# Transposing softmax weights as two halves, moving rows of maxima in one transfer, and planning with other issue times, in a two-layer diffusion transformer

## The chip, the cores and the metric

The kernel runs on one core of a Trainium2 chip. Its time is the device time of one execution in microseconds (us); of several runs the median is given. The engines work in parallel, each through its own instruction stream in order: TensorE (PE, matrix products), VectorE (DVE), ScalarE (ACT, exponentials and copies), GpSimd (POOL, here subtractions and small powers), and SyncE (SP), which in this kernel issues every DMA transfer. The 16 DMA engines then move the data.

## The reference

`BATCH` is 1, `SEQ` 1024 tokens on a 16 x 64 grid, 256 context tokens, width 1024, 16 heads of 64. Layer 0 is grouped-query attention with normed, rotated queries and keys; layer 1 is attention over a window of 8 x 16 neighbours with a learned bias. Each mixer's output is multiplied by a SiLU gate before its output projection. Cut to what this case touches, layer 0 computes, for each block of 128 queries:

```python
q = apply_axial_rope(rms_norm(q, q_g), cos, sin)
k = apply_axial_rope(rms_norm(k, k_g), cos, sin)
k_all = jnp.concatenate([kc, k], axis=1)      # 256 context keys, 1024 token keys
v_all = jnp.concatenate([vc, v], axis=1)
s = jnp.einsum('bqkgd,bskd->bkgqs', qi, k_all).astype(jnp.float32) * ATTN_SCALE
p = jax.nn.softmax(s, axis=-1).astype(v_all.dtype)
o = jnp.einsum('bkgqs,bskd->bqkgd', p, v_all)
yx = (o * jax.nn.silu(z)) @ w_out
```

The input norms are scaled so that scores are large, and a softmax needs the maximum of each query's row before its exponential.

## The kernel before

**Numbers as pairs.** Nearly every operand of a product is kept as two float16 tensors, a high half (the value rounded) and a low half (what the rounding left). A product is then three matmuls: high by high, high by low, low by high.

**Layer 0.** The 16 heads are worked in 8 pairs u. A pair's queries come in five blocks b of two 128-token tiles, and attention in three parts pt: tiles 0 to 3, tiles 4 to 7, and the two context tiles. For pairs 0 to 5 (`QH`) the two heads of a pair take different ways through the token tiles:

- Head 0 (`a_att`) computes scores already transposed, keys by queries (tiles `st`, L1204 and L1205), so that their exponentials (`ph`, `pf` on ACT, the low half `pl` on POOL) are the weights for the value product without a transpose. A query's maximum must then be subtracted inside the product: row 64 of the tile `q2` holds 3 minus the maximum, and row 64 of `k2` holds ones. `mgen` computes the maxima from scores of the high halves (L997, L998), and `rows` brings them into that row: it reduces the partial maxima (L1019), negates them into columns of `zmax` (L1022), transposes that tile by DMA into `zt` (L1023), so that each query tile's maxima are one row of `zt`, and copies rows of `zt` into `q2` (L1027, one transfer per query tile, where only head 0 needs them; L1029, one transfer for all, in the other cases). PE's second score product (L1205) waits for these rows.
- Head 1 (`q_att`) computes scores queries by keys (tile `qs`, L1137 and L1138), so the maximum is a plain reduction (L1140, L1144, L1145). Per query tile t, ACT writes the high half of the weights for 1024 keys into blocks 0 to 7 of the tile `qpp` (L1147) and the exact exponential into `qpf` (L1148); `p_split` writes the low half, their difference, into blocks 8 to 15 on POOL (L1066) or, every sixth time, on VectorE (L1063). One DMA transpose brings the 16 blocks of 128 x 128 into `qpt` (L1151). The value products (L1125 with the high half, L1127 with the low half, alternating key tile by key tile) follow. The 256 context keys go by `qcp` and `qct` (L1154, L1160), four tiles together.

`qpp`, `qpt`, `qcp` and `qct` share six buffers (`y_tile`, tag Y1). Names in the order listings carry u, pt and t: `qpt101` is pair 1, part 0, tile 1; `q211` and `zt11` belong to pair 1, part 1.

**Layer 1** projects queries, keys, values and gates by a scheme of seven products (L1503, L1505), and its window attention transposes weights of 8 or 10 blocks per head and tile (`bph` to `bpht`, L1643).

**What sets the order.** The program text only fixes what depends on what. The class `Planner` then reads all instructions, gives each a cost (`cost`: how long it holds its engine, and how much later its result is there), plays the program through with these costs, and repeats that with due times worked back from PE's stream. The order it ends with is fixed on every engine, SP's queue included; at run time each engine works through its list and waits where an operand is late. For a DMA transpose the cost was 1340 ns of SP whatever its size, and a data time in proportion to its elements.

Of the kernel before, what the change touches and what calls it, by code (L numbers as in the profile page):

```python
# [24 lines left out]
NX = 8  # L25
# [24 lines left out]
class Planner:  # L50
# [42 lines left out]
    def cost(self, x, rd, wr):  # L93
# [4 lines left out]
        n = max([self.elems(a) for a in outs + ins] or [1])  # L98
# [12 lines left out]
        if k == "InstDmaTransposeAnt":  # L111
            m = 1
            for s, c in list(ins[0].ap):
                m *= c
            return 1340.0, m / 128 * 23.4 / 16
        if k == "InstDMACopy":
            m = 1
            for s, c in list(outs[0].ap):
# [391 lines left out]
def trunk_kernel(ctx, tc, x, cx, cc, ng_row, w_mod, w_mod0, b_mod, a_qz, a_kv, a_qg, a_kg, a_w_out,  # L510
                 b_in, tab, b_w_out, fin_g, ones, cos_t, sin_t, out):
    nc = tc.nc
    V, S, G, T, DM = nc.vector, nc.scalar, nc.gpsimd, nc.tensor, nc.sync
# [184 lines left out]
    def y_tile(shape, dt, name, j, at=None):  # L698

        if j == 0:  # L700
            ny[0] += 1
            return main.tile(list(shape), dt, name=name, tag=f"Y0{ny[0] % 2 if at is None else at}", bufs=1)
        return main.tile(list(shape), dt, name=name, tag="Y1", bufs=6)
# [156 lines left out]
    for kt in range(KT):  # L860
# [8 lines left out]
        for t in ((0, 2) if kt < 2 else (0,)):  # L869
            n = 2 if kt < 2 else 4  # L870
# [73 lines left out]
    def a_proj(u, at):  # L944
# [62 lines left out]
        def rows(pts):  # L1007

            zm = zmax[nrow[0] % len(zmax)]
            nrow[0] += 1  # L1010
            zf = aq.tile([P, 16], F32, name=f"zf{u}{pts[0]}", tag="zf", bufs=2)
            zt = aq.tile([P, P], F16, name=f"zt{u}{pts[0]}", tag="zt", bufs=2)
            c0, outs = 0, []
            for pt_ in pts:
                mxs, n = pairs[(u, pt_)][3], PTN[pt_]
                hs = (0,) if pt_ < 2 and u in QH else (0, 1)
                zv = zf[:, c0:c0 + n * len(hs)].rearrange("p (t h) -> p t h", h=len(hs))
                for i in hs:
                    V.tensor_reduce(zv[:, :, i], mxs[i] if pt_ < 2 else mxs[i][:, 0:n, 2:3], axis=AX.X, op=ALU.max)  # L1019
                outs.append((c0, n, len(hs), pairs[(u, pt_)][1]))  # L1020
                c0 += n * len(hs)
            V.tensor_scalar(zm[:, 0:c0], zf[:, 0:c0], -1.0, CSH, op0=ALU.mult, op1=ALU.add)  # L1022
            DM.dma_start_transpose(zt, zm)  # L1023
            for c, n, h, q2 in outs:
                for t in range(n) if h == 1 else (None,):
                    if h == 1:
                        DM.dma_start(q2[64:65, t, 0, :], zt[c + t:c + t + 1])  # L1027
                    else:
                        DM.dma_start(q2[64:65], zt[c:c + n * h])  # L1029
            yield 200  # L1030

        items = []
        for b in range(NT // 2):
            m = (1100 if u in QH else 2200) if b < 4 else 440
            if u == 0:
                v, w, vp, vm, mw = FIRST[b]
            else:
                v = at + 0.2 * b
                w, vp, vm, mw = 0.2, v + 0.29, v + 0.31, 0.2 * m / (1100 if u in QH else 2200)
            items.append((mm(b), v, v + w, 5120))  # L1040
            items.append((post(b), vp, vp + 0.01, 220))
            items.append((mgen(b), vm, vm + mw, m))
            if b in (1, 4):
                items.append((rows((0,) if b == 1 else (1, 2)), vm + mw + 0.01, vm + mw + 0.02, 400))
# [67 lines left out]
    def q_att(u, pt_):  # L1112

        q1, q2, sz, _ = pairs[(u, pt_)]
# [14 lines left out]
        for t in range(4):  # L1129
# [16 lines left out]
            pp = y_tile((P, 2 * NX, P), F16, f"qpp{nm}", 1)  # L1146
# [1 line left out]
            S.activation(pf, pf, AF.Exp, bias=nmx, accum_out=sums[:, t, 0:1])  # L1148
            p_split(pp[:, 0:NX], pp[:, NX:2 * NX], pf, 6)
            ppt = y_tile((P, 2 * NX, P), F16, f"qpt{nm}", 1)  # L1150
            DM.dma_start_transpose(ppt, pp.rearrange("p a b -> p (a b)"))  # L1151
            S.activation(cp[:, t, 0:2], pfc, AF.Exp, bias=nmx)
            S.activation(pfc, pfc, AF.Exp, bias=nmx, accum_out=sums[:, t, 1:2])
            G.tensor_tensor(cp[:, t, 2:4], pfc, cp[:, t, 0:2], op=ALU.subtract)  # L1154
# [787 lines left out]
```

## Time and profile before

| What | Value |
|---|---|
| Runs | 1323.93, 1319.07, 1318.21 us; median 1319.07 us |
| Profiled execution | 1312.96 us, its span 1311.2 us |
| PE busy | 1281.5 us, 98% of the span |
| DVE, ACT, POOL busy | 1025.2, 893.9, 807.4 us |
| DMA | 211.40 MB in 431610 packets; 71.4% of 16 engines' span |
| Granted TensorE clock | 0.999 |

Layer 0's attention lies between about 100 and 640 us of the span, its output projection and the change of layers up to about 800 us, layer 1's attention up to about 1200 us, and the output after that. "Busy" of PE counts a matmul from its start to its modelled end, and matmuls overlap, so short gaps between them do not show. A row of the waits has the waiting instruction, what released it, the total in us, how often, and the longest. SP's transfers appear in the order in which they were issued, with the time of the issue alone; the data land later. Rows of the listings name a tile without its number, so `q<-zt` is a transfer from `zt` into `q2`.

### The profile page before, as it was taken

To read this page: it belongs to the slowest core of one execution; us is meant where nothing else is said; L and a number is where in the kernel's file an instruction comes from. 1 tells how busy PE (TensorE), PEld (TensorE's weight loads), DVE (VectorE), ACT (ScalarE), POOL (GpSimd) and SP (SyncE) were. 2 spreads that over 40 slices of the span, in tenths; PEclk is the share of its full clock that TensorE was granted. 3 is DMA by queue.
4 is the path that set the end of the run, shared out by engine and by line. 5 is a ranking of instruction groups with operands and counts; after the bars stand their busy time and mean duration, and the time that the engine had idled before them with its cause. 6 is when DMAs were issued, how large, how long until landed. Compare 5 with 4: busy or idle time off the path is not lost. (4 is left out here: it accounts for less than half of the span.)

```text
span 1311.2 us, 37092 instructions
## 1 busy us (share of the span) xinstructions
PE 1281.5 (98%) x14503; PEld 899.9 (69%) x14503; DVE 1025.2 (78%) x2410; ACT 893.9 (68%) x1835; POOL 807.4 (62%) x1030
## 2 busy tenths in 40 slices
PE   9999999999999999999999999999999999999997
PEld 6458777777777777767654466778696777868543
DVE  4787788798979798969658896778888788788743
ACT  3672797788878887778864345777878677777611
POOL 1572787677687876768864883556665555553432
PEclk9999999999999999999999999999999999999999
DMA  9422478778788886884406795789798887979923
GB/s 371 162 82 72 99 142 167 134 179 170 140 161 184 153 164 145 168 213 124 137 34 181 209 165 175 136 172 182 148 182 167 165 188 138 195 155 236 244 97 113
DMA packets 431610, 211.40 MB, mean 161 GB/s; under 512 B 386697, under 2 KB 390601, under 8 KB 431433
## 3 DMA queue, kind: packets, MB, share of 16 engines
q1 hardware_dynamic: 431434, 209.04, 71.4%
q8 instruction: 113, 1.85, 0.6%
q14 instruction: 63, 0.52, 0.1%
HBM read 97.23 MB, written 14.71 MB: 85 GB/s over the span
## 5 line engine op out<-in xcount | busy, mean ns | idle before, releaser
L1066 POOL TENSOR_TENSOR pl<-pf,ph 128x256 f16<-128x256 f32 x340 | 239.4, 728 | 66.6 <-ACT pf L1191 51.8
L1066 POOL TENSOR_TENSOR bph<-bpf,bph 128x256 f16<-128x256 f32 (+1 forms) x172 | 148.9, 890 | 184.4 <-ACT bpf L1640 122.9
L967 PE MATMUL pa<-wa,x 128*128 128x256 f16 x1536 | 216.5, 272 | 0.4 <-DVE mrow L626 0.2
L967 PEld LDWEIGHTS <-x 128*128 128x128 f16 x1536 | 141.8, 97 | 35.6 <-issue 1.8
L1189 ACT ACTIVATE ph<-st 128x512 f16<-128x512 f32 x200 | 118.7, 605 | 64.0 <-PE st L1205 53.3
L998 DVE TENSOR_REDUCE mxp<-pm 128x1 f32<-128x512 f32 x160 | 107.7, 683 | 14.6 <-PE pm L997 13.0
L1191 ACT ACTIVATE pf<-st 128x512 f32<-128x512 f32 x200 | 119.0, 610 | 0.2 <-POOL pl L1066 0.2
L1066 POOL TENSOR_TENSOR qpp<-qpf,qpp 128x512 f16<-128x512 f32 x84 | 96.4, 1168 | 30.0 <-ACT qpf L1148 23.2
L1639 ACT ACTIVATE bph<-bpf,bnx 128x640 f16<-128x640 f32 (+1 forms) x128 | 96.4, 794 | 26.6 <-DVE bnx L1634 25.9
L1505 PEld LDWEIGHTS <-wb 128*128 128x128 f16 x672 | 61.3, 98 | 68.1 <-issue 4.9
L1073 PE MATMUL pv<-v,ph 128*128 128x64 f16 x800 | 104.7, 195 | 0.0
L1072 PE MATMUL pv<-v,ph 128*128 128x65 f16 x800 | 104.1, 193 | 0.0
L1074 PE MATMUL pv<-v,pl 128*128 128x65 f16 x800 | 103.5, 192 | 0.1
L1640 ACT ACTIVATE bpf<-bpf,bnx 128x640 f32<-128x640 f32 (+1 forms) x128 | 101.3, 792 | 0.2
L1503 PEld LDWEIGHTS <-s 128*128 128x128 f16 x1536 | 87.0, 98 | 4.9 <-issue 3.7
L1072 PEld LDWEIGHTS <-ph 128*128 128x128 f16 x800 | 75.9, 97 | 19.9 <-issue 0.5
L1073 PEld LDWEIGHTS <-ph 128*128 128x128 f16 x800 | 75.5, 97 | 13.8 <-issue 0.2
L1074 PEld LDWEIGHTS <-pl 128*128 128x128 f16 x800 | 76.2, 99 | 9.4 <-POOL pl L1066 0.8
L1204 PE MATMUL st<-q,k 128*128 128x512 f16 x200 | 75.4, 379 | 3.8 <-ACT pf L1191 3.6
L1205 PE MATMUL st<-q,k 65*128 65x512 f16 x200 | 74.9, 380 | 3.1 <-DMA q<-zt 3.0
L1468 POOL TENSOR_TENSOR tsb<-wsb 128x256 f32<-128x256 f32 x64 | 52.5, 841 | 31.2 <-DMA wsb<-in_b_in 23.3
L1140 DVE CUSTOM_DVE_ANT_0 qpf<-qs,zero 128x512 f32<-128x512 f32 x96 | 65.6, 684 | 6.0 <-PE qs L1138 2.7
(549 smaller groups left out, 3889.4 us busy)
## 6 DMA issues: line engine op xcount, KB each, us to landing
wg<-in_w_mod SPq DMA_DIRECT2D x64, 256.0 KB
wsb<-in_b_in SPq DMA_DIRECT2D x64, 256.0 KB
tb<-in_tab SPq DMA_DIRECT2D x16, 576.0 KB
wm<-in_w_mod SPq DMA_DIRECT2D x16, 512.0 KB
wsa<-in_a_qz SPq DMA_DIRECT2D x32, 256.0 KB
xstage<-in_x SPq DMA_DIRECT2D x8, 512.0 KB
wsoa<-in_a_w_out SPq DMA_DIRECT2D x16, 256.0 KB
x<-in_x SPq DMA_DIRECT2D x8, 512.0 KB
```

Of the source, the lines that this page charges most:

```text
L967: T.matmul(ps[:, :, i, :], hA(a, kt, t), wt[w][:, kt, :], start=n == 0, stop=n == 3 * KT - 1)
L998: V.tensor_reduce(mxs[i][:, t, ch:ch + 1], pm, axis=AX.X, op=ALU.max)
L1066: G.tensor_tensor(lo[:, c], p32[:, c], hi[:, c], op=ALU.subtract)
L1072: T.matmul(pv[:, t, :], hi[:, c], v[:, 0:65], start=first and t == 0, stop=False)
L1073: T.matmul(pv[:, t, 0:HD], hi[:, c], v[:, 65:129], start=False, stop=False)
L1074: T.matmul(pv[:, t, :], lo[:, c], v[:, 0:65], start=False, stop=last and t == n - 1)
L1189: S.activation(ph, st, AF.Exp)
L1191: S.activation(p32, st, AF.Exp)
L1204: T.matmul(so, k1[:, g, kc], q1[:, :, i, :], start=True, stop=False)
L1503: T.matmul(ps[:, t], a_blk(a, kt, m)[:, t], w[kt][:, b, WIX[m]], start=f, stop=l, skip_group_check=not first)
L1639: S.activation(ph, pf[:, 0:k_], AF.Exp, bias=m)
L1640: S.activation(pf[:, 0:k_], pf[:, 0:k_], AF.Exp, bias=m, accum_out=sums[:, t - t0, i:i + 1])
```

## The change

Three edits. In `rows`, the transfers of single rows of `zt` into `q2` for head 0 (4 per part, 48 in all) become one transfer per part (12 in all), in the form that the other cases already have. In `q_att`, the transpose of 16 blocks becomes two of 8 blocks each: blocks 0 to 7, which hold the high half, and blocks 8 to 15, which hold the low half; 48 transfers become 96, of the same bytes together. In `Planner.cost`, the issue time of a DMA transpose becomes the larger of 1340 ns and its elements divided by 102.4: 1340 ns up to 8 blocks, 1600 ns for 10 blocks, 2560 ns for 16. No computation differs. Line numbers fall by four behind the first edit and by two behind the second: L1151 becomes L1149, L1160 becomes L1158, L1643 becomes L1641.

```diff
--- before.py
+++ after.py
@@ -112,7 +112,7 @@
             m = 1
             for s, c in list(ins[0].ap):
                 m *= c
-            return 1340.0, m / 128 * 23.4 / 16
+            return max(1340.0, m / 102.4), m / 128 * 23.4 / 16
         if k == "InstDMACopy":
             m = 1
             for s, c in list(outs[0].ap):
@@ -1022,11 +1022,7 @@
             V.tensor_scalar(zm[:, 0:c0], zf[:, 0:c0], -1.0, CSH, op0=ALU.mult, op1=ALU.add)
             DM.dma_start_transpose(zt, zm)
             for c, n, h, q2 in outs:
-                for t in range(n) if h == 1 else (None,):
-                    if h == 1:
-                        DM.dma_start(q2[64:65, t, 0, :], zt[c + t:c + t + 1])
-                    else:
-                        DM.dma_start(q2[64:65], zt[c:c + n * h])
+                DM.dma_start(q2[64:65, :, 0, :] if h == 1 else q2[64:65], zt[c:c + n * h])
             yield 200
 
         items = []
@@ -1148,7 +1144,9 @@
             S.activation(pf, pf, AF.Exp, bias=nmx, accum_out=sums[:, t, 0:1])
             p_split(pp[:, 0:NX], pp[:, NX:2 * NX], pf, 6)
             ppt = y_tile((P, 2 * NX, P), F16, f"qpt{nm}", 1)
-            DM.dma_start_transpose(ppt, pp.rearrange("p a b -> p (a b)"))
+            for a in range(2):
+                sl = slice(a * NX, (a + 1) * NX)
+                DM.dma_start_transpose(ppt[:, sl], pp[:, sl].rearrange("p a b -> p (a b)"))
             S.activation(cp[:, t, 0:2], pfc, AF.Exp, bias=nmx)
             S.activation(pfc, pfc, AF.Exp, bias=nmx, accum_out=sums[:, t, 1:2])
             G.tensor_tensor(cp[:, t, 2:4], pfc, cp[:, t, 0:2], op=ALU.subtract)
```

All five engines get another order in layer 0, from pair 0's second half on; SP's order in layer 1 is the old one but for some neighbours exchanged. Three places follow.

SP, the rows of maxima of pair 1, part 1. Before:

```order
L984 DMA_TRANSPOSE q120_3213<-q16q20_3429 128x4x128
L1023 DMA_TRANSPOSE zt11_3438<-zmax1_1309 128x128
L986 DMA q220_3214<-q120_3213 64x512
L1027 DMA q211_2271<-zt11_3438 1x16x8 x4
L1029 DMA q212_2837<-zt11_3438 1x4x128
L1151 DMA_TRANSPOSE qpt101_3389<-qpp101_3384 128x16x128
L1083 DMA_TRANSPOSE oa0_2377<-ol01_3083 128x8x128
L1151 DMA_TRANSPOSE qpt102_3534<-qpp102_3529 128x16x128
L1108 DMA oa_d_1304<-oa0_2377 128x2048
```

SP there now (two rows of the same tile `qpt` are its high and then its low half):

```order
L984 DMA_TRANSPOSE q120_3212<-q16q20_3430 128x4x128
L1149 DMA_TRANSPOSE qpt101_3389<-qpp101_3384 128x8x128
L1023 DMA_TRANSPOSE zt11_3439<-zmax1_1309 128x128
L1149 DMA_TRANSPOSE qpt102_3532<-qpp102_3527 128x8x128
L1079 DMA_TRANSPOSE oa0_2375<-ol01_3082 128x8x128
L1025 DMA q211_2269<-zt11_3439 1x4x128
L1149 DMA_TRANSPOSE qpt101_3389<-qpp101_3384 128x8x128
L1149 DMA_TRANSPOSE qpt102_3532<-qpp102_3527 128x8x128
L984 DMA_TRANSPOSE q120_3212<-q16q21_3716 128x4x128
L611 DMA wg025601_3746<-in_w_mod 128x512
L1025 DMA q212_2835<-zt11_3439 1x4x128
```

The four single rows into `q211` are one transfer, and its place has moved: ahead of it stand the high half of tile 102 and the transpose of `oa0`; the whole transposes of tiles 101 and 102 stood behind the rows before, and their low halves still do.

ACT around the exponentials of tiles 101 and 102 (L1147 before, L1143 now, are those that write the high half). Before:

```order
L1147 ACTIVATE qpp101_3384<-qpf101_3305,qnx101_3381 128x1024
L1189 ACTIVATE ph1008_3608<-st1008_3605 128x512
L1148 ACTIVATE qpf101_3305,qsm10_3204<-qpf101_3305,qnx101_3381 128x1024
L1191 ACTIVATE pf1008_3610<-st1008_3605 128x512
L1189 ACTIVATE ph1009_3649<-st1009_3646 128x512
L973 ACTIVATE th21_3703<-pa21_3432 128x256
L1191 ACTIVATE pf1009_3651<-st1009_3646 128x512
L1152 ACTIVATE qcp10_3205<-qpc101_3306,qnx101_3381 128x256
L1081 CAST ol01_3083<-og01_2388 128x512
L748 ACTIVATE sq1_936<-pa21_3432 128x4x64
L1153 ACTIVATE qpc101_3306,qsm10_3204<-qpc101_3306,qnx101_3381 128x256
L1147 ACTIVATE qpp102_3529<-qpf102_3475,qnx102_3526 128x1024
```

ACT there now:

```order
L1143 ACTIVATE qpp101_3384<-qpf101_3305,qnx101_3381 128x1024
L1150 ACTIVATE qcp10_3204<-qpc101_3306,qnx101_3381 128x256
L1144 ACTIVATE qpf101_3305,qsm10_3203<-qpf101_3305,qnx101_3381 128x1024
L748 ACTIVATE sq1_936<-pa21_3433 128x4x64
L1151 ACTIVATE qpc101_3306,qsm10_3203<-qpc101_3306,qnx101_3381 128x256
L1143 ACTIVATE qpp102_3527<-qpf102_3473,qnx102_3524 128x1024
```

Ten rows stood between the two exponentials of the high half, and four do now; head 0's exponentials (`ph`, `pf`) and the copy `ol01` are elsewhere.

SP, tiles 110 and 111 of pair 1. Before:

```order
L1160 DMA_TRANSPOSE qct10_3800<-qcp10_3205 128x16x128
L984 DMA_TRANSPOSE q121_3719<-q16q22_4012 128x4x128
L1023 DMA_TRANSPOSE zt20_4157<-zmax0_1308 128x128
L1151 DMA_TRANSPOSE qpt110_3935<-qpp110_3930 128x16x128
L1027 DMA q220_3214<-zt20_4157 1x16x8 x4
L986 DMA q221_3720<-q121_3719 64x512
L1151 DMA_TRANSPOSE qpt111_4074<-qpp111_4069 128x16x128
L984 DMA_TRANSPOSE q121_3719<-q16q23_4282 128x4x128
```

SP there now:

```order
L1158 DMA_TRANSPOSE qct10_3800<-qcp10_3204 128x16x128
L1149 DMA_TRANSPOSE qpt103_3681<-qpp103_3676 128x8x128
L1149 DMA_TRANSPOSE qpt110_3935<-qpp110_3930 128x8x128
L984 DMA_TRANSPOSE q121_3719<-q16q22_4013 128x4x128
L1023 DMA_TRANSPOSE zt20_4159<-zmax0_1308 128x128
L1149 DMA_TRANSPOSE qpt111_4075<-qpp111_4070 128x8x128
L1149 DMA_TRANSPOSE qpt110_3935<-qpp110_3930 128x8x128
L1025 DMA q220_3213<-zt20_4159 1x4x128
L986 DMA q221_3720<-q121_3719 64x512
L1149 DMA_TRANSPOSE qpt111_4075<-qpp111_4070 128x8x128
```

The high half of tile 111 stands ahead of the low half of tile 110, and the rows of maxima into `q220` stand behind both; before they stood behind tile 110 alone.

## The prediction

> **What bounds the kernel now.** I read the page first, then the table of stretches, then who waited for whom. The page:
>
> ```profile
> span 1311.2 us, 37092 instructions
> PE 1281.5 (98%) x14503; PEld 899.9 (69%) x14503; DVE 1025.2 (78%) x2410; ACT 893.9 (68%) x1835; POOL 807.4 (62%) x1030
> ```
>
> TensorE (PE) is busy for all but 1311.2 - 1281.5 = 29.7 us, and no other engine comes near it. The change takes no matmul away, so a gain can only come out of these 29.7 us (and out of short gaps that the modelled ends of matmuls hide), and a loss can only be new idle time of PE. The stretches show where the idle time lies; the first two columns are the stretch and its length, the third is PE's busy time:
>
> ```profile
> 0.00:100.00 100.00, 95.55 (x670) 56.61 (x671) 68.38 (x167) 58.89 (x124) 46.10 (x68) 1.00 0.54 202
> 100.00:640.00 540.00, 525.40 (x6573) 401.72 (x6571) 456.27 (x1240) 415.29 (x862) 391.26 (x495) 1.00 0.72 151
> 640.00:800.00 160.00, 158.15 (x1242) 87.35 (x1240) 113.94 (x164) 75.19 (x141) 103.28 (x118) 1.00 0.62 152
> 800.00:1200.00 400.00, 398.94 (x5261) 297.97 (x5260) 325.54 (x712) 301.81 (x618) 226.70 (x308) 1.00 0.84 168
> 1200.00:1311.00 111.00, 103.46 (x769) 56.23 (x763) 61.11 (x128) 42.69 (x95) 40.02 (x42) 0.99 0.62 161
> ```
>
> PE idles 4.5 us in the opening, 14.6 us in layer one's attention (100 to 640), 1.9 us between the layers, 1.1 us in layer two's attention (800 to 1200) and 7.5 us at the end. The granted clock is 0.99 to 1.00 throughout and has no part in this. Every edited line of the kernel works in the 540 us that hold the 14.6. What PE waits for there:
>
> ```profile
> PE qpv L1125 <- DMA qpt<-qpp: 5.2, 6, 1.1
> PE st L1204 <- ACT pf L1191: 3.6, 4, 2.1
> PE st L1205 <- DMA q<-zt: 3.0, 5, 1.0
> PE bpv L1647 <- DMA bpht<-bph: 1.1, 1, 1.1
> PE pmc L1003 <- DMA q<-q16q: 0.9, 1, 0.9
> ```
>
> The first and the third row are the two transfers that the change rewrites: 5.2 us in six waits for transposed softmax weights (qpt), 3.0 us in five waits for the row of negated maxima (zt). Together 8.2 us, or 0.6% of the span, are what the change aims at. The 3.6 us on ScalarE (ACT) and the 0.9 us are outside it.
>
> **The rows of maxima.** Four transfers of one row each become one of four rows. What each costs SP, the engine that issues all transfers (minimum, median, maximum in ns), the transposes beside them:
>
> ```profile
> L1027 SPq DMA_DIRECT2D q<-zt x48: 553/587/1882, 125.3 to 500.9; - x48
> L1029 SPq DMA_DIRECT2D q<-zt x12: 616/666/991, 156.1 to 642.3; - x12
> L1151 SPq DMA_TRANSPOSE qpt<-qpp x48: 1504/2076/5031, 136.7 to 550.2; - x48
> L1083 SPq DMA_TRANSPOSE oa<-ol x14: 1231/1256/1864, 193.5 to 632.1; - x14
> L1023 SPq DMA_TRANSPOSE zt<-zmax x16: 1126/1182/2008, 122.2 to 637.8; - x16
> ```
>
> The new form exists already as L1029. Per group 4 x 0.587 = 2.35 us of issue become 0.67; twelve groups give SP 12 x 1.68 = 20 us back. What that is worth to PE is read at one of the five waits (pair 1, first half; SP's queue, then PE):
>
> ```profile
> 214.45 1.20 SPq L1023 DMA_TRANSPOSE zt<-zmax  x1
> 215.74 0.55 SPq L986 DMA_DIRECT2D q<-q  x1
> 216.85 3.35 SPq L1027 DMA_DIRECT2D q<-zt  x4
> 220.24 0.66 SPq L1029 DMA_DIRECT2D q<-zt  x1
> 221.01 1.87 SPq L1151 DMA_TRANSPOSE qpt<-qpp  x1
> 221.43 0.38 PE L1205 MATMUL st<-q,k 65*128 65x512 f16 x1 [0.89 <-DMA q<-zt]
> ```
>
> PE came at 221.43 - 0.89 = 220.54 and started 1.23 us after the fourth issue ended (216.85 + 3.35 = 220.20). With one issue at the same place it could start at 216.85 + 0.67 + 1.23 = 218.75, and the wait would be gone; the same 2.7 us cover all five waits, the longest of which is 1.0 us. So the full gain is -3.0 us. But the transfer does not keep its place. In the new order of SP shown ahead, two transposes now stand between zt and its rows: the first half of tile 102 (pair 1, half 0, block 2), which waits for that tile's exponential on ACT, and oa0. In the old run that exponential is the second of these rows (its first is tile 101's):
>
> ```profile
> 213.06 1.15 ACT L1147 ACTIVATE qpp<-qpf,qnx 128x1024 f16<-128x1024 f32 x1 [1.58 <-DVE qnx L1145]
> 219.09 1.17 ACT L1147 ACTIVATE qpp<-qpf,qnx 128x1024 f16<-128x1024 f32 x1
> ```
>
> If ACT kept this time, the rows would be issued at 220.26 + 2 x 1.256 = 222.8 and reach PE at 222.8 + 0.67 + 1.23 = 224.7, 4.1 us after it asked: 3.3 us worse than now at this place. ACT does not keep it: between the two exponentials stood 10 other rows of ACT's order and now 4 (shown ahead too), so 6.03 us / 11 x 5 = 2.7 us instead of 6.0, which puts the rows at PE at about 221.4, where they are now. The two ends are -3.0 us (all five waits gone) and +3.3 us (one such place goes wrong); counted in the order, a half of a weight tile stands between zt and its rows for 11 of the 12 groups, where before a whole tile stood there for 5, and for 2 more between some of the four rows. I take half of the gain, -1.5 us.
>
> **The two halves.** The high half of a weight tile needs only ACT's exponential (L1147), the low half also POOL's or VectorE's subtraction (L1066, L1063). One tile of the old run (110: pair 1, second half, block 0) and the next one's exponential:
>
> ```profile
> 239.72 1.17 ACT L1147 ACTIVATE qpp<-qpf,qnx 128x1024 f16<-128x1024 f32 x1
> 242.96 2.28 POOL L1066 TENSOR_TENSOR qpp<-qpf,qpp 128x512 f16<-128x512 f32 x2 [2.00 <-PE qs L1138]
> 246.34 1.18 SPq L1023 DMA_TRANSPOSE zt<-zmax  x1
> 247.69 1.99 SPq L1151 DMA_TRANSPOSE qpt<-qpp  x1
> 247.00 1.15 ACT L1147 ACTIVATE qpp<-qpf,qnx 128x1024 f16<-128x1024 f32 x1 [0.74 <-DMA qct<-qcp]
> 253.80 0.23 PE L1125 MATMUL qpv<-v,qpt 128*128 128x128 f16 x1 [1.10 <-DMA qpt<-qpp]
> ```
>
> The data were ready at 242.96 + 2.28 = 245.24; SP, still at other transfers, issued at 247.69, and PE got the tile 6.11 us later and had waited 1.10 us. After the split, 8 blocks instead of 16 are left to move once the subtraction is done. No row shows these halves' landing, but the oa transposes are of the same 8 blocks: 1.256 us of issue, 0.73 us under today's 1.99. If only the issue shrinks, the low half lands 6.11 - 0.73 = 5.4 us after its issue; if the data time (6.11 - 1.99 = 4.12) halves too, 1.256 + 2.06 = 3.3 us. But here as well the order has changed: the high half of the next tile, 111, now stands ahead of this low half. On the old times it may start when that tile's exponential ends, at 248.15, and takes 1.26 us, so the low half goes out at 249.4 and PE has it between 252.7 and 254.8, against 253.80: from 1.1 us better to 1.0 us worse. Of the 48 low halves, 9 stand behind a later tile's high half in this way; 30 directly follow their own high half, and for those nothing stands in the way of the gain. Ends for the term: -5.2 us (all six waits gone) and 9 x 1.0 = +9 us (all nine on the wrong side). The row nearest to the typical place is the 8-block transpose, 1.256 us; I take a little over half of the gain, -3.0 us.
>
> By the Trainium skill (Perfetto Trace Analysis, DMA Optimizations) splitting a transfer lets parts start sooner if the DMA engines are generally idle. Here their share is 0.72 over layer one's attention, so its condition is not met; by that rule this term would be 0 and the sum -1.5 us.
>
> **SP's own time.** Two halves cost 2 x 1.256 = 2.51 us of issue. Against the median of 2.08 that is 48 x 0.44 = +21 us, against the minimum of 1.504 it is +48 us, against the 20 us that the rows give back; below nothing it cannot go far, since even one block costs 1.182. I take the median: 21 - 20 = +1 us of SP. SP can carry it, because it stands waiting in the same stretch, for POOL alone:
>
> ```profile
> SPq L1151 <- POOL pl L1066: 60.5, 27, 6.4
> ```
>
> That is 60.5 us ahead of these very transposes. The cover for this term is that wait; at +28 us half of it would be used and nothing would yet reach PE. Term: 0.
>
> **The new issue times.** The rule max(1340, elements / 102.4) changes nothing for transposes up to 8 blocks (1340 ns), adds 260 ns to those of 10 blocks in layer two and makes qct's 16 blocks 2560 ns. This edits no instruction; it moves rows. In layer two SP's order is almost what it was (a few neighbours exchanged), and PE idles 1.1 us in 400 there: ends -1.1 and, for a single exchange of the size of the one DMA wait seen there, +1.1 us; term 0. In layer one all five engines have a new order, and the other 14.6 - 8.2 = 6.4 us of idle time are dealt again; with nothing to favour a side the ends are about half of it either way, +/-3 us, term 0.
>
> **Sum:** -1.5 - 3.0 + 0 + 0 = -4.5 us on the profiled execution, whose own time is 1312.96 us (its span and 1.8 us around it): 1308.5 us. The timed runs shown have a median of 1319.07, 6.1 us above the profiled one and with none below 1318.21; I carry the difference over to them: 1314.6 us.
>
> **Rivals.**
> (1) The waits are only dealt again: 0 us, 1319 us. For it: 11 of 12 row transfers now have halves ahead of them, and the DMA share of 0.72. Against: 30 of 48 low halves follow their own high half at once.
> (2) Slower: high halves in front block SP. SP works in order; a high half that waits for an exponential holds back low halves and rows that are ready. The nine low halves behind a later tile cost 9 x 1.0 = 9 us, less some of the rows' gain: +8 us, 1327 us. It decides from the point where, at several places, the next tile's exponential ends more than about 1.9 us after the low half is ready: PE asked for tile 110 at 253.80 - 1.10 = 252.70, and 252.70 - 4.35 (the middle of the two landing times) - 1.26 = 247.1, against 245.24. For it: tile 110 above, where 248.15 - 245.24 = 2.9 us. Against: the new order brings exponentials together as well, at tiles 101 and 102.
> (3) A larger gain, -10 us, 1309 us: with smaller pieces in SP's queue the 0.9 us on q16q and the 3.6 us on ACT shrink as well, and 10 of the 14.6 us go. For it: SP is behind in several of the waits, as at 245.24 to 247.69. Against: the longest of the ACT waits is 2.1 us, and PE waits there for an exponential that no transfer feeds.
>
> **Numbers.** The forecast (-4.5 us, its own range 1310 to 1318) gets 0.46, rival 1 0.19, rival 2 0.18, rival 3 0.17. About 0.5%, 6.6 us, is what a measurement of this kernel can tell from no change. Faster by more: all of rival 3 and a third of the forecast, 0.17 + 0.15 = 0.32. Slower by more: most of rival 2 and a trace of rival 1, 0.18. Between: 0.50. The range of 8 in 10 runs from 1307 (most of rival 3 inside) to 1325 (part of rival 2 outside).
>
> **What would show it.** Right: PE's busy time in 100 to 640 us up from 525.4 of 540 (with a stretch some 4 us shorter), the waits of L1125's successor on qpt under 2.5 us in total, those on zt near 1.5; SP's median for a half near 1.26 us; layer two's 400 us as full as now. Wrong for the rows: waits on zt as long as before, with SP's wait for ACT right ahead of them. Wrong for the halves: PE waiting on qpt where SP issued another tile's high half first. Wrong for SP: halves at 1.5 us and more each and no wait for POOL left. The forecast falls as a whole if the idle time of the opening, the end or layer two moves by more than 3 us, because no term above reaches there.

## The result, and the profile after

| | before | after |
|---|---|---|
| Median of 5 runs | 1320.66 us | 1311.40 us |
| Lowest to highest | 1318.21 to 1323.93 us | 1308.34 to 1313.66 us |
| Ratio after / before | | 0.9942, 95% interval 0.9922 to 0.9962 |
| Profiled execution | 1312.96 us | 1313.66 us |

The change makes the kernel faster by 0.6%, some 7.6 us of 1319. The two profiled executions hide this: that of before is a fast one (6 us under the median of the runs beside it, and not one of the five), that of after is the slowest of its five. Their pages therefore show what changed in kind; where the time went is read below from two new profiles taken on one chip. In the runs further down, two executions lie far outside all others, one of the faster version (5129 us) and one of the kernel before beside it (2662 us), and enter no ratio. After, its page:

```profile
span 1311.9 us, 37092 instructions
PE 1283.3 (98%) x14503; PEld 901.0 (69%) x14503; DVE 1025.6 (78%) x2410; ACT 894.2 (68%) x1835; POOL 803.2 (61%) x1030
```

Its stretches (layer one's attention and layer two's; PE's busy time is the third number):

```profile
100.00:640.00 540.00, 528.37 (x6591) 403.48 (x6589) 458.47 (x1239) 416.29 (x862) 389.40 (x498) 1.00 0.74 152
...
800.00:1200.00 400.00, 397.84 (x5245) 297.08 (x5243) 323.93 (x712) 300.26 (x615) 225.77 (x308) 1.00 0.83 168
```

In 100 to 640 us PE idles 11.6 us instead of 14.6; layer two is about as full as before (2.2 us of idle time instead of 1.1). What PE waits for in 100 to 640 us (total in us, times, longest):

```profile
PE qpv L1123 <- DMA qpt<-qpp: 3.8, 3, 2.1
PE qs L1133 <- DVE mxp L998: 2.2, 2, 1.6
...
PE qpv L1121 <- DMA qpt<-qpp: 0.8, 1, 0.8
PE st L1202 <- ACT pf L1189: 0.8, 2, 0.5
...
PE st L1203 <- DMA q<-zt: 0.3, 1, 0.3
```

The waits for the rows of maxima (`zt`) are nearly gone, from 3.0 to 0.3 us. Those for weight tiles (`qpt`) went only from 5.2 to 4.6 us here. SP's queue: the issue of a half (minimum, median, maximum in ns), and the longest waits ahead of the halves in the same stretch:

```profile
L1149 SPq DMA_TRANSPOSE qpt<-qpp x96: 1231/1264/2958, 135.1 to 555.0; - x96
```

```profile
SPq L1149 <- POOL pl L1062: 19.1, 16, 4.0
SPq L1149 <- ACT qcp L1150: 16.9, 12, 5.5
```

A half costs 1.264 us of issue at the median, as forecast from the oa transposes. SP's wait for POOL ahead of the weight tiles fell from 60.5 us to 19.1; the halves now also wait for ACT.

### The profile page after: what moved, and what is told of

Same layout as the page of the kernel before. It is cut to its first block, busy times and chain, and to the rows that moved or that the text cites. A ratio compares the mean times of both kernels' runs of the same rounds, so it can differ in the third digit from the quotient of the medians.

```text
span 1311.9 us, 37092 instructions
## 1 busy us (share of the span) xinstructions
PE 1283.3 (98%) x14503; PEld 901.0 (69%) x14503; DVE 1025.6 (78%) x2410; ACT 894.2 (68%) x1835; POOL 803.2 (61%) x1030
## 4 chain that ended last, share of the span: by engine, by line
PE 78%; DVE 10%; DMA 4%; ACT 4%; issue 3%; POOL 1%; SPq 0%; POOLq 0%; DVEq 0%; ACTq 0%
PE pa L967 12%; PE poa L1295 7%; PE pob L1799 5%; PE bsa L1619 4%; PE pkv L834 3%; PE bpv L1645 2%; PE st L1203 2%; PE st L1202 2%; DVE mxp L998 2%; PE pm L997 2%; PE qpv L1121 2%; PE qs L1133 1%; PE qs L1134 1%; PE pv L1069 1%; PE pv L1070 1%
## 5 line engine op out<-in xcount | busy, mean ns | idle before, releaser
L1062 POOL TENSOR_TENSOR pl<-pf,ph 128x256 f16<-128x256 f32 x340 | 232.4, 707 | 68.1 <-ACT pf L1189 46.8
L1070 PEld LDWEIGHTS <-pl 128*128 128x128 f16 x800 | 76.2, 99 | 10.5 <-POOL pl L1062 2.2
```

What stands on the lines that cost most here:

```text
L1062: G.tensor_tensor(lo[:, c], p32[:, c], hi[:, c], op=ALU.subtract)
L1070: T.matmul(pv[:, t, :], lo[:, c], v[:, 0:65], start=False, stop=last and t == n - 1)
```

## The experiments

Each kernel was timed over five rounds beside the kernel before on the same chip; ratios are to those runs. The first four share a chip, so do the next four; the two with transfers into a scratch tile and the faster version share a third, and the run between them is on a fourth. A number that compares kernels of different chips sets two such ratios against each other, and the difference of two has an interval of some 0.25% to either side. "The old order" means that every engine's order is not planned anew but taken from the kernel before and held as a table; its edit is always

```diff
-        plan.schedule(margin=100.0)
-        plan.refine(5, 100.0, 300.0)
+        plan.order = planned()
```

together with the edits of the transfers that are named.

### The kernels themselves, on one chip

No edit: the kernel before and the kernel after, run once more as if they were new.

> The kernel before, unchanged, beside its own runs: what two sets of runs of one program differ by, and a profile of it on the chip of the other three. Every theory: ratio 1.000 within 0.003. Its PE waits for qpt and zt should again be near 5.2 and 3.0 us; if they differ by 2 us or more from one execution to the next, single waits of one profile cannot carry a term of the sum.

> The changed kernel once more, on the same chip as the other three. My theory (the transfers themselves: the waits of PE for qpt and zt shrink) and its rival (a new order of all five engines) both expect the recorded ratio, 0.992 to 0.996. The profile beside that of the kernel before on this chip should show 5 to 9 us less in the 540 us of layer one's attention and the same layer two.

Measured: before 1318.60 us, ratio 1.0008 [0.9995, 1.0022]; after 1308.74 us, ratio 0.9934 [0.9918, 0.9950]. What can be told from no change here is some 0.2%. PE's waits in 100 to 640 us, before:

```profile
PE st L1204 <- ACT pf L1191: 5.2, 4, 3.5
PE qpv L1125 <- DMA qpt<-qpp: 5.0, 7, 1.1
PE st L1205 <- DMA q<-zt: 2.6, 4, 1.2
PE pm L997 <- DVE mxp L998: 1.3, 2, 0.8
```

and after:

```profile
PE qs L1133 <- DVE mxp L998: 2.2, 2, 1.6
PE qpv L1123 <- DMA qpt<-qpp: 1.4, 2, 0.9
PE pm L997 <- DVE mxp L998: 1.3, 3, 0.5
PE qpv L1121 <- DMA qpt<-qpp: 0.9, 1, 0.9
...
PE st L1202 <- ACT pf L1189: 0.4, 1, 0.4
```

The end of layer one's attention is well marked by the first product of the output projection (`poa`; the two times at the end of the row are its first and last start), before and after:

```profile
L1297 PE MATMUL poa<-woa,oar x288: 377/379/380, 632.8 to 745.0; 128*128 128x512 f16 x144
```

```profile
L1295 PE MATMUL poa<-woa,oar x288: 377/379/380, 623.3 to 736.4; 128*128 128x512 f16 x144
```

So 9.5 us of the 11.2 us between the two spans (1318.1 and 1306.9) are won before the output projection begins. The waits on qpt and zt give 5.3 us of it (7.6 to 2.3), those on ACT's `pf` another 4.8, and 2.2 go back to a new wait for VectorE's maxima (L1133). That is 7.9 us. The 1.6 us left, and more, are the granted clock: in the kernel before, the longest wait (3.5 us, for `pf`) ends at 587.96 us, and behind it the clock stands at half (the column before the last two):

```profile
588.00:590.00 2.00, 2.00 (x14) 1.25 (x14) 2.00 (x4) 1.87 (x4) 1.29 (x2) 0.50 0.34 66
590.00:592.00 2.00, 2.00 (x16) 1.20 (x14) 1.36 (x3) 1.03 (x3) 1.31 (x2) 0.50 0.46 139
592.00:594.00 2.00, 2.00 (x15) 1.38 (x14) 0.92 (x2) 1.05 (x3) 0.91 (x2) 0.62 0.58 160
```

A product over 512 columns takes up to 0.63 us there instead of 0.38. By these rows some 2.8 us are lost (an estimate: 2 x 0.50 + 2 x 0.50 + 2 x 0.38); the kernel after has no such place in layer one in this profile. Smaller waits and gaps take about 1 us back.

### Both new transfers in the old order, and the new issue times alone

The first has the two edits of the transfers as in the change, at the places that their forerunners had (the four rows at the place of the first of four, the low half right behind the high half). The second has only the new line in `cost`, and the order that follows from it:

```diff
-            return 1340.0, m / 128 * 23.4 / 16
+            return max(1340.0, m / 102.4), m / 128 * 23.4 / 16
```

> The two kinds of new transfers, but every engine keeps the order of the kernel before: the single transfer of four rows stands where the first of the four stood, the low half directly behind the high half where the whole transpose stood. Transfers as the cause: PE's waits for zt (3.0 us) gone and those for qpt (5.2 us) half gone, the time 4 to 6 us shorter, ratio 0.995 to 0.997. New order as the cause: nothing or at most 2 us, ratio 0.999 to 1.001, the gain needs the order.

> The transfers of the kernel before, the order planned with issue times that count blocks. Transfers as the cause: no gain, 0 +/- 3 us by the waits being dealt again, ratio 0.998 to 1.002. Issue times as the cause (the old order took 16-block transposes for 1340 ns where 2076 are measured, and SP ran behind its plan): most of the gain already here, 5 us or more, ratio under 0.996.

Measured: both transfers in the old order 1310.68 us, ratio 0.9946 [0.9926, 0.9966]; the new issue times alone 1318.66 us, ratio 1.0002 [0.9985, 1.0019]. The transfers are the cause. The new issue times without them do nothing that can be told, and the new order adds 0.1% to the transfers, less than can be told (the two intervals together leave anything from -0.1 to 0.4%). The rival that the waits are only dealt again falls. But the two orders do not win in the same places: in the old order PE still waits 5.6 us for ACT's `pf`, the longest 4.0, and the clock drops behind that wait as it does in the kernel before.

### Each transfer alone

The rows alone:

```diff
-                for t in range(n) if h == 1 else (None,):
-                    if h == 1:
-                        DM.dma_start(q2[64:65, t, 0, :], zt[c + t:c + t + 1])
-                    else:
-                        DM.dma_start(q2[64:65], zt[c:c + n * h])
+                DM.dma_start(q2[64:65, :, 0, :] if h == 1 else q2[64:65], zt[c:c + n * h])
```

The halves alone:

```diff
-            DM.dma_start_transpose(ppt, pp.rearrange("p a b -> p (a b)"))
+            for a in range(2):
+                sl = slice(a * NX, (a + 1) * NX)
+                DM.dma_start_transpose(ppt[:, sl], pp[:, sl].rearrange("p a b -> p (a b)"))
```

> Edit: the order of every engine is the old kernel's; only the four single-row transfers of a group become one transfer of four rows, at the place of the first of the four. Weight tiles go whole. Theory (each transfer removes its own waits): the waits of PE on the row of negated maxima, 2.6 us in four in the run of the kernel before on this study's chip, go, those on the weight tiles (5.0 us in seven) stay: ratio 0.998, about -2.6 us. Rival A (the gain is that of a less crowded SP queue, 20 us of issue time given back): the waits on the weight tiles shrink too, -5 us or more, ratio 0.996 or lower. Rival B (the rows are hidden anyway): ratio 1.000, and the whole gain belongs to the halves.

> Edit: the old order again; only the weight tiles' transpose is cut in two, high half and then low half, at the place of the whole one. Rows of maxima go one by one. Theory (each its own waits): the waits on weight tiles, 5.0 us in seven, go: -5 us, ratio 0.996; together with the rows alone this adds up to the -7.2 us (ratio 0.9946) of both transfers in the old order. Rival A (SP time decides): the halves alone cost SP 48 x 0.44 = 21 us with no rows to pay for them, the later rows of maxima come later, and the gain is under 2 us, ratio 0.9985 or above; the two parts alone then give less than the two together.

Measured: the rows alone 1309.32 us, ratio 0.9929 [0.9912, 0.9946]; the halves alone 1316.96 us, ratio 0.9993 [0.9977, 1.0009]. My theory fell in both: in the old order the rows give everything, the halves nothing that can be told. With the rows alone PE's waits in 100 to 640 us are

```profile
PE st L1200 <- ACT pf L1187: 5.3, 4, 3.8
PE qpv L1121 <- DMA qpt<-qpp: 2.4, 3, 1.4
PE pm L997 <- DVE mxp L998: 0.8, 2, 0.5
```

The waits for weight tiles were halved although nothing about weight tiles was edited. With the halves alone:

```profile
PE qpv L1127 <- DMA qpt<-qpp: 5.2, 8, 1.1
PE st L1206 <- ACT pf L1193: 5.0, 4, 3.4
PE st L1207 <- DMA q<-zt: 1.7, 2, 1.5
```

These waits are as long as before, but have moved: L1127 is the product with the low half, where in the kernel before PE stopped at L1125, the high half. The high half is there in time, but for one wait of 0.4 us, and the low half is not.

Why a transfer of maxima moves a wait for weights can be seen in SP's queue. The kernel before (SP's issues, start and length):

```profile
322.95 4.72 SPq L1151 DMA_TRANSPOSE qpt<-qpp  x1
327.78 2.47 SPq L1027 DMA_DIRECT2D q<-zt  x4
330.35 1.83 SPq L1151 DMA_TRANSPOSE qpt<-qpp  x1
```

The same place with the rows alone:

```profile
318.49 3.90 SPq L1147 DMA_TRANSPOSE qpt<-qpp  x1
322.49 0.64 SPq L1025 DMA_DIRECT2D q<-zt  x1
323.23 1.81 SPq L1147 DMA_TRANSPOSE qpt<-qpp  x1
```

The next weight tile goes out 0.84 us after the one in front has been issued (322.39), where it was 2.68 us (327.67). At each of the twelve places in layer one the rows' issue is shorter by some 1.7 us (4 x 0.587 less 0.669, by the medians); where SP is behind, as here, whatever stands behind them goes out that much earlier.

### The low half first

As both transfers in the old order, with the two halves exchanged in SP's part of the table:

```diff
-SP: ... transpose of blocks 0 to 7, transpose of blocks 8 to 15 ...
+SP: ... transpose of blocks 8 to 15, transpose of blocks 0 to 7 ...
```

> Edit: as the run with both new transfers in the old order, but the low half is issued before the high half. The number, the sizes and the place of the transfers stay; what goes is the early start of the high half, which now waits in SP's order until the subtraction has made the low half ready. Theory (the gain of the halves is the early start: one half is already under way while the subtraction runs): the gain of the halves is lost, or turns to a loss since two issues now stand behind the subtraction instead of one: ratio 0.998 or above. Rival (the gain is that smaller pieces land faster): ratio as with the high half first, 0.9946.

Measured: 1310.83 us, ratio 0.9946 [0.9927, 0.9964], the ratio of the high half first. PE's largest wait for weights is now on the high half (L1121), as it should be:

```profile
PE qpv L1121 <- DMA qpt<-qpp: 3.2, 7, 1.0
```

In the old order, then, the early start of the high half is worth nothing that the times can tell. In the profiles it is worth 2.0 us: PE's waits for weights come to 1.2 us in 100 to 640 us with the high half first and to 3.2 us here, 0.15% of the time, where the two intervals are 0.2% to either side. That so little comes of it fits the halves' result, since PE needs the low half directly behind the high one.

### Four rows again, in the new order

The kernel after with its own order as a table and its halves, but with the old lines of `rows`; the four transfers stand at the place of the one:

```diff
-                DM.dma_start(q2[64:65, :, 0, :] if h == 1 else q2[64:65], zt[c:c + n * h])
+                for t in range(n) if h == 1 else (None,):
+                    if h == 1:
+                        DM.dma_start(q2[64:65, t, 0, :], zt[c + t:c + t + 1])
+                    else:
+                        DM.dma_start(q2[64:65], zt[c:c + n * h])
```

> Edit: the changed kernel with its own new order and its halves, but the row of maxima goes again as four transfers of one row, at the place of the one. Theory (each its own waits): the waits on the row of maxima come back, +2.6 us on the changed kernel, ratio to the kernel before 0.9955. Rival A (in the new order the rows are issued early enough, so their number is hidden): no change against the changed kernel, ratio 0.9935. Rival B (SP's queue is the limit): 12 x 1.68 = 20 us more of SP time push the halves back as well, +5 us or more, ratio 0.997 or above.

Measured: 1328.58 us, ratio 1.0073 [1.0056, 1.0091], so slower than the kernel before, and 1.4% (0.0139 of 1319 us, 18 us) above the kernel after. Rival B held, and more strongly than it said. Most of the added waiting is not for the rows but for the weight tiles behind them (10.5 us where the kernel after waited 2.3):

```profile
PE qpv L1127 <- DMA qpt<-qpp: 8.9, 10, 2.0
PE st L1207 <- DMA q<-zt: 2.0, 2, 1.5
PE qpv L1125 <- DMA qpt<-qpp: 1.6, 1, 1.6
```

A part of the 18 us is again the clock: it was 0.992 to 0.994 in five of the six runs of this kernel, and 0.999 in all six of the kernel after. Over 1320 us a clock lower by 0.5% is some 7 us (an estimate).

Whether the halves win anything in the new order was not tested: no run has the new order with merged rows and whole tiles.

### SP's issue time by itself

The new theory was that the rows' gain is the issue time that SP gets back. Two kernels give SP transfers that nobody needs, `junk` being a scratch tile. The first merges the rows and spends the time again, at the places of the other three:

```diff
+    junk = aq.tile([P, P], F16, name="junk", bufs=1)
+    njunk = [0]
...
+                DM.dma_start(q2[64:65, :, 0, :] if h == 1 else q2[64:65], zt[c:c + n * h])
+                if h == 1:
+                    for t in range(1, n):
+                        k = njunk[0]
+                        njunk[0] += 1
+                        DM.dma_start(junk[k:k + 1], zt[c + t:c + t + 1])
```

The second leaves the four single rows as they are and adds the same loop behind them. Both are in the old order.

> Edit: the old order, whole weight tiles, one transfer of four rows at the place of the first of four; at the places of the other three SP issues three transfers of one row each into a scratch tile that nobody reads. So all four rows still arrive early, but SP spends the same issue time as the old kernel (12 x 3 x 0.59 = 21 us given back by the merging are spent again). Theory, formed on the runs so far (the gain of the rows is SP's issue time: what stands behind them in its queue, above all weight tiles, goes out 1.7 us earlier): most of the gain goes; the waits on weight tiles come back to about 5 us, only those on the row of maxima stay away: ratio 0.998 or above. Rival (the gain is the earlier arrival of the rows themselves): ratio stays at 0.993, waits on weight tiles near 2.4 us as with the rows alone.

> Edit: the kernel before, in its order, and behind the last of the four single-row transfers of each of the twelve groups three more of the same size into a scratch tile that nobody reads: 36 x 0.59 = 21 us more of SP's issue time, while rows and weight tiles are made as before. Theory (SP's issue time is on the path in layer one): it costs about as much as taking the same time away gave, 7 to 10 us, with longer waits on weight tiles: ratio 1.006. Rival (SP's time is covered by its 60 us of waits for POOL, as the prediction said): ratio 1.000 to 1.002.

Measured: rows merged with the issue time kept 1315.28 us, ratio 0.9989 [0.9970, 1.0008]; the old kernel with more issue time 1333.46 us, ratio 1.0138 [1.0102, 1.0174]. The first has all its rows early, and of its gain of 0.71% only 0.11% is left. The second costs more than I expected, 1.38% or 18 us for 36 transfers; of these some 4 us are a lower clock (a mean of 0.994 in its runs against 0.997 in those of the kernel before, an estimate as above). The transfers into the scratch tile, and PE's waits for weights, in the first and in the second:

```profile
L1032 SPq DMA_DIRECT2D junk<-zt x36: 550/582/1849, 126.7 to 503.0; - x36
...
PE qpv L1128 <- DMA qpt<-qpp: 8.9, 11, 1.8
```

```profile
L1036 SPq DMA_DIRECT2D junk<-zt x36: 587/589/1541, 127.2 to 514.9; - x36
...
PE qpv L1132 <- DMA qpt<-qpp: 15.6, 13, 2.7
```

So 36 x 0.58 = 21 us of SP's time in layer one are worth 0.60% (8 us) between the rows alone and the first kernel, and 1.38% (18 us) between the kernel before and the second. In the second the weight tiles' own issue rose too, from a median of 2.05 us to 2.38, so that its dose is rather 21 + 48 x 0.33 = 37 us; in the first it did not (2.02 and 2.03). An added transfer takes a place in the DMA queue as well as SP's time, and these runs do not separate the two. The prediction held that SP's waits for POOL cover this. Those waits ahead of the weight tiles, in the kernel before, with the rows alone, in the first and in the second:

```profile
SPq L1151 <- POOL pl L1066: 63.5, 28, 6.6
```

```profile
SPq L1147 <- POOL pl L1062: 62.5, 22, 6.6
```

```profile
SPq L1154 <- POOL pl L1069: 62.3, 26, 6.2
```

```profile
SPq L1158 <- POOL pl L1073: 58.4, 24, 6.7
```

They stay near 60 us in all four, while the medians run from 1309 to 1333 us. These waits absorb hardly any of the added issue time. Others take up a part: all of SP's waits from 100 us to the first product of the output projection fall by 13 us from the rows alone to the first kernel (316.7 to 303.5) and by 30 us from the kernel before to the second (302.1 to 271.8). The rest comes where SP is behind.

### The issue time that the halves were reckoned to cost, without the halves

The rows alone in the old order, and behind three of every four whole weight tiles one transfer into the scratch tile:

```diff
             DM.dma_start_transpose(ppt, pp.rearrange("p a b -> p (a b)"))
+            if njunk[0] % 4 != 3:
+                k = njunk[0]
+                DM.dma_start(junk[k:k + 1], pp[64:65, NX, :])
+            njunk[0] += 1
```

> Edit: the rows alone in the old order (weight tiles go whole), and behind the transpose of three of every four weight tiles one more transfer of one row into a scratch tile that nobody reads: 36 x 0.59 = 21 us of SP's issue time, as much as cutting the tiles in two was reckoned to cost, without the smaller pieces. The run with both new transfers in the old order (halves and rows) stood at 0.9946, the rows alone at 0.9929. Theory (the halves do land earlier, and pay for it with issue time that is on the path): without the smaller pieces the issue time alone costs 8 to 18 us, as it did behind the rows: ratio 0.999 to 1.006. Rival (behind the weight tiles SP's time is covered, and smaller pieces are worth nothing): ratio as with the halves, 0.993 to 0.996.

Measured: 1315.31 us, ratio 0.9988 [0.9971, 1.0005], just under the lower edge of the theory and outside the rival's range. Issue time behind weight tiles is not fully covered either: it costs 0.59% against the rows alone. But the dose was larger than meant:

```profile
L1152 SPq DMA_DIRECT2D junk<-qpp x36: 575/924/1350, 138.6 to 537.9; - x36
...
L1149 SPq DMA_TRANSPOSE qpt<-qpp x48: 1562/2474/4602, 136.1 to 544.8; - x48
```

The added transfers took 0.92 us at the median, and the whole tiles' own issue rose too, from 2.02 us with the rows alone to 2.47: 36 x 0.92 + 48 x 0.46 = 55 us, where the halves of the run with both transfers cost 96 x 1.284 - 48 x 2.016 = 26.5 us. The run shows that the cost exists, and that it is small for its dose: 7.8 us for 55. The added transfer also reads `qpp`, whose buffer could come free later for it; the profile has no wait that is put down to that. It does not measure how much the halves' smaller pieces give back: by this run anything from nothing to 0.42% (0.9988 - 0.9946).

### A faster version

With the rows alone the longest wait of PE left in layer one is one for ACT (3.8 us). Followed back, ACT stands in its own queue before a cast of output weights whose load SP issued late:

```profile
575.13 0.63 ACT L678 ACTIVATE woa<-wsoa 128x512 f16<-128x512 f32 x1 [3.19 <-DMA wsoa<-in_a_w_out]
```

The edit is in SP's part of the order table alone:

```diff
-SP: ... oc<-ol5c, wg x3, wsoa, wsoa, oar<-oa_d, wsoa, ...
+SP: ... wsoa, wsoa, oc<-ol5c, wsoa, wg x3, oar<-oa_d, ...
```

> Edit: the rows alone in the old order (the best run so far, ratio 0.9929), and on SP three loads of layer one's output weights go out earlier: two ahead of the transpose of oc and one behind it, instead of behind three loads of modulation weights. Nothing else moves. With the rows alone ScalarE waited 3.19 us for these loads at 571.9 to 575.1 us, and TensorE behind it 3.8 us for an exponential's input at 579. Theory: that wait shrinks to about 1 us and the kernel gains 3 us: ratio 0.9905. Rival (another wait takes its place, the modulation weights now late, or the end of layer one waits for something else): no change, ratio 0.993.

Measured: 1304.24 us, ratio 0.9906 [0.9877, 0.9935], as the theory said, and the lowest median of all. ACT finds the same operand ready:

```profile
572.09 0.63 ACT L678 ACTIVATE woa<-wsoa 128x512 f16<-128x512 f32 x1
```

PE's waits for ACT's `pf` fall to this, the clock is lowered nowhere in 100 to 640 us (with the rows alone it fell to 0.50 right behind the wait of 3.8 us), and the output projection starts at 617.9 us:

```profile
PE st L1200 <- ACT pf L1187: 1.9, 4, 0.7
...
L1293 PE MATMUL poa<-woa,oar x288: 377/380/380, 617.9 to 730.5; 128*128 128x512 f16 x144
```

Against the kernel after, the two ratios (0.9906 and 0.9934) are 0.28% apart with intervals that overlap, from runs on different chips; that it beats the kernel before is shown, that it beats the kernel after is likely.

## Why the prediction was right or wrong

**The number and the sign** were right: 1314.6 us forecast, 1311.4 measured, inside the range and inside the forecast's own range. The size was too small: -4.5 us against about -7.6 (0.58%), closer to the rival of -10. The working behind it was right only in part: it counted 3.0 us for the halves, which gave nothing that can be told, and nothing for SP's time, which gave most. That the errors partly offset each other is luck.

**What bounds the kernel.** Right. PE's idle time in layer one was where the gain came from (9.5 of 11.2 us on one chip), and PE's idle time in layer two moved by no more than 1.4 us. Two things were left out. The clock has a part: over 540 us it stayed at 0.99 to 1.00, but some 2.8 us of the 9.5 are the half clock behind the kernel before's longest wait, which its first profile did not have. And the waits on ACT's `pf`, put outside the change, fell from 3.6 to 0.8 us in the first pair of profiles and from 5.2 to 0.4 in the second; with the new transfers in the old order they stay, at 5.3 us (rows alone) and 5.6 (both), so it is the new order that removes them. Against the transfers in the old order it still wins no more than can be told.

**Rows of maxima, -1.5 us.** The term was meant for the rows' earlier arrival at PE, and as that it was about right: with the rows merged and SP's time kept, 0.11%, 1.4 us, with an interval that includes nothing. In that kernel's profile PE's waits on zt are gone, and those on weight tiles have grown (8.9 us against 5.0). The term's upper bound of +3.3 us, a half standing between zt and its rows, did not come: waits on zt nearly vanished in the new order.

**The two halves, -3.0 us.** Wrong for the old order, where it could be tried: -0.07% with four rows, and 0.9946 against 0.9929 with the rows merged, neither to be told from nothing. The step that failed is the one that let the low half land earlier because 8 blocks are left after the subtraction and took a little over half of the waits for it. The kernel with the halves alone waits as long as before, at the low half. In the kernel after the place that I had worked out (tile 110, whose low half stands behind tile 111's high half) came out as its bad end. SP, and PE's wait:

```profile
247.92 2.62 SPq L1149 DMA_TRANSPOSE qpt<-qpp  x2
250.64 0.69 SPq L1025 DMA_DIRECT2D q<-zt  x1
```

```profile
254.93 0.20 PE L1123 MATMUL qpv<-v,qpt 128*128 128x64 f16 x1 [2.07 <-DMA qpt<-qpp]
```

PE waited 2.07 us for the low half where it had waited 1.10 for the whole tile, 1.0 us worse as the working's upper end said, and from 256 to 260 us the clock stood near half (0.52 and 0.63 in two slices of 2 us), which costs 1.7 us more. In the second profile of the kernel after no wait for weights is longer than 0.9 us, so it is a place that tips over, not a steady cost.

By the Trainium skill (Perfetto Trace Analysis, DMA Optimizations) splitting may let the whole finish sooner if the DMA engines are generally idle; it gives no share that counts as idle. Their share was 0.72 in this stretch, and the split paid nothing that can be told: the 0 that I had read from the rule was nearer than my -3.0. The runs here cannot say whether the engines' share is the reason, or the issue time of the added pieces.

**SP's own time, 0.** This is the step that failed most. I added 21 us for the halves and took off 20 us for the rows, and called the net of +1 us covered by 60.5 us of SP's waits for POOL. In truth the 20 us given back are the largest term of all: 0.60% or 8 us (the rows alone against the rows with their issue time kept), and in the new order even 18 us (four rows against one; some 7 of them by the clock). The cover was not one: these waits stayed near 60 us whatever was added, since a sum of waits over 540 us says nothing on the places where SP is behind. The prediction's own row showed such a place: tile 110's data were ready at 245.24, and SP, busy with other transfers, issued it at 247.69. What I used there as a delay of one tile was the general case.

By the Trainium skill (DMA: Bandwidth & Descriptors, Issuing engines are not separate DMA queues) the issuing engine's time per transfer is usually small beside the transfer. Here it is not: a row's issue took 0.58 us, and PE started 1.23 us after the end of the last one; 36 added transfers of this kind cost 8 to 18 us.

**New issue times, 0.** Right: ratio 1.0002.

**The rivals.** That the waits are only dealt again: no, the gain stays with every engine in its old order. Slower, because high halves block SP: no, but its idea that SP works in order and holds back what is ready was the right one, with the single rows as what blocks. The larger gain, -10 us: its size was nearly met. Its cause, "smaller pieces in SP's queue", was not: what helped was fewer issues, not smaller pieces. That the waits on ACT shrink came as it said, by the new order.

**What would show it.** SP's 1.26 us per half and the full layer two came as written. PE's busy time in 100 to 640 us rose from 525.40 to 528.37 us in the first pair of profiles and from 523.97 to 530.54 us on one chip. The waits on qpt under 2.5 us: 2.3 us on one chip, 4.6 in the first profile. Those on zt fell below the 1.5 us, to 0.3 and to none. The sign against the halves came too, in the first profile: PE waiting at tile 110, where SP had issued another tile's high half first. These signs were met by a mechanism that the list did not separate from mine; only each transfer alone did.

## What to carry to other kernels

An engine that issues transfers in order can be on the path wherever its queue is behind, and a large sum of waits for other engines elsewhere in the same stretch need not cover added issue time; ask at each wait of the bounding engine when the operand's data were ready and when its transfer was issued, and what stood in the queue between. Where it is behind, many small transfers are worth merging even if nobody waits for them: in this case their price was paid by what was queued behind them. And when two edits have opposite costs on such a queue, try each alone, because one may carry the whole gain.

## What was not expected of the hardware

- Issue time on SP's queue was worth far more than its cover suggested, and very differently by place: per us of SP's issue 0.1 us of the end behind weight tiles (7.8 us for 55), 0.4 behind merged rows (8 us for 21), 0.5 in the old kernel with more issue time (18 us for 37) and 0.9 with four rows in the new order (18 us for 20). Whether it is the 0.58 us of issue itself, or the transfer's place ahead of the next transpose in the DMA queue, was not separated.
- A long wait of PE cost more than its length where the clock fell behind it: to 0.50 for some 3 to 6 us after waits of 3.54 us (kernel before, second profile), 4.01 us (both transfers in the old order), 3.79 us (rows alone) and 2.07 us (kernel after, first profile). It did not fall behind the longest wait of the kernel before's first profile, 2.1 us, so these profiles give no length at which it begins.
- The issue time of the same transpose is no constant: 16 blocks took a median of 2.02 us with the rows alone, 2.05 in the kernel before, 2.38 in the old kernel with 36 more small transfers, and 2.47 with 36 small transfers directly behind them; the small ones took 0.58 us behind others of their kind and 0.92 behind a large transpose.
